# The low parts of eight weight tiles are made on GpSimd instead of VectorE, ahead of the output projection of a hybrid mixer

## The chip, the cores and the metric

The kernel runs on one core of a Trainium2 chip. A core has five engines that each work through their own list of instructions in order: TensorE (PE in the profile; PEld is its loading of weights), VectorE (DVE), ScalarE (ACT), GpSimd (POOL) and SyncE (SP), which here only starts transfers. They wait for each other by semaphores. The metric is the device time of one execution in microseconds, the median of several runs.

## The reference, cut to what matters

The reference is a decoder trunk of two layers for 512 tokens of width 1024. A layer is a SwiGLU block, a mixer and a second SwiGLU block, each with a scaled residual and a layer norm behind it:

```python
def hybrid_mixer(xn, w_in, conv_w, ..., w_out, lambda_init):
    qa, ka, va, qb, kb, vb, qkv_c, z_c, beta_c, a_c = jnp.split(xn @ w_in, points, axis=-1)
    ...
    oa = rms_norm(oa, diff_norm_g) * (1.0 - lambda_init)      # differential attention, 4 heads
    ob = rms_norm(ob, sb_norm_g)                              # stick-breaking attention, 4 heads
    oc = gated_delta_rule(l2_normalize(heads(qc, C_HEADS)), l2_normalize(heads(kc, C_HEADS)), ...)
    oc = rms_norm(oc, dn_norm_g) * jax.nn.silu(heads(z_c, C_HEADS).astype(jnp.float32))
    o = jnp.concatenate([tokens(oa), tokens(ob), tokens(oc)], axis=-1)
    return o @ w_out

    def step(state, inp):                                     # inside gated_delta_rule
        v_new = u_i - jnp.einsum('bhck,bhkv->bhcv', w_i, state)
        out = jnp.einsum(... q_i * exp(g_i), state) + jnp.einsum('bhcs,bhsv->bhcv', a_i, v_new)
        state = state * jnp.exp(g_last)[..., None] + jnp.einsum(... v_new)
        return state, out
```

The step carries a state from chunk to chunk and cannot run ahead of itself. The kernel uses chunks of 128 tokens, so there are four.

## The kernel before

All activations lie with features on the 128 partitions and the 512 tokens beside each other, as eight tiles of 128x512. Products with weights keep float32 accuracy with three passes: weights and activations are each split into a rounded high part and a low part (the rest), and `mm3` adds high times high (L103), high times low (L104) and low times high (L105).

`Stream.get` brings the weights. A transfer fetches eight blocks of 128x128 (`wraw`, two buffers); every four blocks are then split into `whi` by ScalarE (L89, a copy that rounds) and `wlo` (L90, a subtraction of two tensors in SBUF). Which engine runs L90 is decided by

```python
(eng or self.eng or nc.vector).tensor_tensor(out=lo, in0=r, in1=hi.bitcast(F32), op=ALU.subtract)
```

`st.eng` is None through the SwiGLU blocks, so DVE does it there. In the mixer it is set to `nc.gpsimd` after the first projections (L538) and, in the kernel before, set back to None at L1030, just before the output projection. The tiles come from the pools `ws` (six buffers) and `wx` (two at this point; its space is free only when the mixer's early pools are closed, L1031).

The mixer runs, in the order in which the code is written: projections and stick-breaking attention, projections of the delta rule with their convolution, the triangular inverses (`triangles`, `delta`), differential attention (`attend(0, 0)` and `attend(0, 1)`, units of scores L880/L881, softmax on ACT and DVE, L904 transposes, L909 products, and `finish` L948 to L966 with `turned` L972/L975 behind it), then `outputs`, which transposes the operands of the delta rule (`operands`, L758 and L763) and runs the scan. `gate` projects z and `split` (L994 on ACT, L995) makes high and low parts of the four attention outputs on GpSimd and of the four outputs of the delta rule on DVE; `nm.residual` adds the residual's high and low parts (L134, GpSimd).

The scan (`state`) works on two pairs of heads in turn. A step (`scan`) is L773 (PE), L775 (DVE), L779 (PE), L781 (DVE), L786 (PE), L792 (DVE, the new state; L789 in the first chunk), and L797 and L798 for the output, copied out by L840 (ACT). Its PSUM tiles come from a pool of two banks (`pa`). After every second chunk `emit` normalises a pair's outputs: L810 on ACT, then on DVE L814, L815, L816, a reciprocal root (L111, and three times L114, L115, L116 on tiles of 128x4 named `orr_t` and `of`), L818 and L819; a transpose (L824) follows at the next step. `finish` uses the same root (`arr_t`, `af`) for the attention.

The output projection (`project_norm` with `head`) works on four tiles of outputs first with the four attention parts as inputs, which can begin during the scan, then with the four parts of the delta rule; the low parts for these come by L90 of the first eight `get` groups. `nm.add` (L151 to L168) sums what the layer norm needs.

The order of instructions is not the order of the code. A scheduler places each engine's instructions by its own model of their durations, and an engine then keeps to that list. Thus an instruction that moves to another engine changes the lists of the others too.

Of the kernel before, what the change touches and what calls it, by code (L numbers as in the profile page):

```python
# [98 lines left out]
def mm3(g, out, w, x, first, last):  # L99
    nc = g.nc  # L100
    whi, wlo = w
    xhi, xlo = x
    nc.tensor.matmul(out=out, lhsT=whi, rhs=xhi, start=first, stop=False)  # L103
    nc.tensor.matmul(out=out, lhsT=whi, rhs=xlo, start=False, stop=False)  # L104
    nc.tensor.matmul(out=out, lhsT=wlo, rhs=xhi, start=False, stop=last)  # L105
# [321 lines left out]
def mixer(g, l):  # L427
    nc = g.nc
    st = g.st
# [12 lines left out]
    def pd():  # L442
        return g.pd.tile([P, T], F32, name="pd")

    def py():
        return psc.tile([P, T], F32, name="psc")
# [580 lines left out]
        nm.residual(d)  # L1027


    st.eng = st.queue = None  # L1030
    early.close()  # L1031
    g.more_weights()
    st.use([g.ws] * WS, [g.wx] * 2)
# [16 lines left out]
    def head():  # L1050

        tiles = [pd(), pd(), py(), py()]
        for a, b in ((0, 4), (4, KD)):
            for d, p in enumerate(tiles):
                for i in range(a, b):
                    mm3(g, p, st.get(bo + d * KD + order[i]), parts[i], i == 0, i == KD - 1)
                if b == KD:
                    for i in range(0, KD, PC):
                        st.get(bo + (d + 4) * KD + i)
                    nm.add(d, p, 0, T)  # L1060
            if b < KD:
                for d in range(4):
                    st.get(bo + d * KD + PC)
                st.use([g.ws] * 3 + [g.wx] * 5)

    def ahead(*pools):
# [6 lines left out]

    nxt = [st.at + i * PC for i in range(2 * NF)]
    project_norm(g, nm, ksum, False, 4, ((0, ahead(g.ws, g.ws, g.ws)), (KD, ahead(g.ws, g.ws)), (2 * KD, ahead(g.ws, g.wx)), (3 * KD, ahead(g.wx))), head, bank)
    ctx.close()


def program(ctx, tc, a, out, mixer=None):
# [101 lines left out]
    for l in range(DEPTH):  # L1181
        ffn(g, 3 * l, False, True)
        if mixer:
            mixer(g, l)
        ffn(g, 3 * l + 2, l == DEPTH - 1, False)
# [73 lines left out]
```

## Time and profile before

| | us |
|---|---|
| median of three runs | 2250.42 (2246.45 to 2251.85) |
| the profiled execution | 2250.16 |
| its span, first to last instruction | 2248.4 |
| PE busy | 2138.2 (95%) |
| DVE busy | 1169.6 (52%) |
| ACT busy | 907.9 (40%) |
| POOL busy | 377.5 (17%) |

The span of 2248.4 us holds both layers one after the other. The busy shares are means over stages with different limits; what a stage waits for is seen in the timelines, where a row has the start in us, the time that its instructions took, their line, operation and tiles, and, in brackets, the idle time of the engine before it with what ended that.

### The profile page before, as it was taken

The numbers are of one execution on the slowest core, as the hardware profiler recorded it, in microseconds if no ns is written. First come the engines' busy times: TensorE is split into PE (matmuls) and PEld (weight loads), VectorE is DVE, ScalarE is ACT, GpSimd is POOL, SyncE is SP. The second block draws the span as 40 slices with busy tenths as digits, with TensorE's granted clock in tenths as the row PEclk, the third lists the DMA queues.
The fourth block names the chain that finished last, engine by engine and source line by source line (L and its number), as shares of the span: only waits on it lengthen the run. The fifth ranks groups of instructions, "written<-read, shape, count | busy, mean of one in ns | idle before, by whom it ended". The sixth has DMA issues, their size and how long they took to land. (4 is left out here: it accounts for less than half of the span.)

```text
span 2248.4 us, 30132 instructions
## 1 busy us (share of the span) xinstructions
PE 2138.2 (95%) x11382; PEld 1782.6 (79%) x11382; DVE 1169.6 (52%) x2363; ACT 907.9 (40%) x1801; POOL 377.5 (17%) x327
## 2 busy tenths in 40 slices
PE   8999999999798999999999999999987989999997
PEld 7888889777677888888888888897776768888886
DVE  4533436386578833343663334263774788333426
ACT  4333324575464533332443333245753535333313
POOL 1100011426204400000130000023461234000010
PEclk9999999999899999999999999999998999999998
DMA  6423323514512233332333333234144123333322
GB/s 190 125 94 95 98 75 104 139 40 122 129 58 72 84 109 94 94 94 75 116 109 95 94 94 94 66 104 131 57 133 109 48 85 94 95 96 100 95 66 94
DMA packets 90898, 217.32 MB, mean 97 GB/s; under 512 B 21968, under 2 KB 36336, under 8 KB 90752
## 3 DMA queue, kind: packets, MB, share of 16 engines
q1 hardware_dynamic: 82848, 187.47, 27.5%
q10 hardware_dynamic: 6912, 25.17, 3.8%
q0 software_dynamic: 992, 2.75, 0.7%
q8 instruction: 90, 1.47, 0.3%
q14 instruction: 56, 0.46, 0.1%
HBM read 193.83 MB, written 6.83 MB: 89 GB/s over the span
## 5 line engine op out<-in xcount | busy, mean ns | idle before, releaser
L89 ACT CAST whi<-wraw 128x512 fp32r<-128x512 f32 x692 | 421.4, 619 | 959.4 <-PE pd L104 755.1
L90 DVE TENSOR_TENSOR wlo<-wraw,whi 128x512 fp32r<-128x512 f32 x580 | 431.0, 751 | 658.6 <-ACT whi L89 647.4
L103 PE MATMUL pd<-x,whi 128*128 128x512 f32 (+1 forms) x1920 | 726.7, 380 | 12.9 <-ACT x L1177 6.2
L105 PE MATMUL pd<-x,wlo 128*128 128x512 f32 (+1 forms) x1920 | 728.3, 380 | 3.2 <-DVE wlo L90 3.2
L104 PE MATMUL pd<-x,whi 128*128 128x512 f32 (+1 forms) x1920 | 727.7, 379 | 1.6 <-POOL x L231 1.3
L103 PEld LDWEIGHTS pd<-x,whi 128*128 128x128 f32 x1920 | 365.8, 191 | 77.5 <-ACT x L1177 6.2
L105 PEld LDWEIGHTS pd<-x,wlo 128*128 128x128 f32 x1920 | 366.2, 191 | 67.4 <-DVE wlo L90 3.4
L104 PEld LDWEIGHTS pd<-x,whi 128*128 128x128 f32 x1920 | 366.2, 191 | 66.8 <-POOL x L231 3.0
L103 PE MATMUL pd<-hhi,whi 128*128 128x512 f32 (+1 forms) x880 | 307.7, 350 | 0.0
L104 PE MATMUL pd<-hlo,whi 128*128 128x512 f32 (+1 forms) x880 | 307.7, 350 | 0.0
L105 PE MATMUL pd<-hhi,wlo 128*128 128x512 f32 (+1 forms) x880 | 307.3, 349 | 0.0
L168 POOL TENSOR_TENSOR lt<-lt 128x512 f32<-128x512 f32 x26 | 38.9, 1497 | 1065.3 <-ACT lt L165 1065.3
L103 PEld LDWEIGHTS pd<-hhi,whi 128*128 128x128 f32 x880 | 165.5, 188 | 24.4
L105 PEld LDWEIGHTS pd<-hhi,wlo 128*128 128x128 f32 x880 | 165.4, 188 | 24.1
L104 PEld LDWEIGHTS pd<-hlo,whi 128*128 128x128 f32 x880 | 165.5, 188 | 24.1
L90 POOL TENSOR_TENSOR wlo<-wraw,whi 128x512 fp32r<-128x512 f32 x112 | 150.2, 1357 | 138.7 <-ACT whi L89 70.1
L259 DVE TENSOR_TENSOR lt<-pd,lt 128x512 f32<-128x512 f32 x88 | 60.4, 689 | 111.9 <-PE pd L105 110.7
L231 POOL TENSOR_TENSOR x<-x 128x256 fp32r<-128x256 f32 x60 | 45.1, 753 | 162.5 <-ACT x L229 132.7
L134 POOL TENSOR_TENSOR x<-x 128x512 f32<-128x512 f32 x48 | 70.9, 1522 | 0.0
L261 DVE TENSOR_TENSOR hlo<-lt,hhi 128x512 fp32r<-128x512 f32 x88 | 67.0, 765 | 6.3
L165 ACT ACTIVATE lt<-x 128x256 f32<-128x256 f32 (+1 forms) x58 | 29.7, 512 | 95.8 <-DVE x L163 95.5
L568 DVE SCALAR_TENSOR_TENSOR kqv<-pd,conv,kqv 128x511 f32<-128x511 f32 (+2 forms) x72 | 53.5, 743 | 20.1 <-ACT kqv L566 18.9
(309 smaller groups left out, 2287.9 us busy)
## 6 DMA issues: line engine op xcount, KB each, us to landing
wraw<-in_w SPq DMA_DIRECT2D x308, 512.0 KB, 3.5
wraw<-in_w ACTq DMA_DIRECT2D x48, 512.0 KB, 3.6
kqv<-kqv SPq DMA_DIRECT2D x128, 64.0 KB, 2.0
kqv<-kqv SPq DMA_DIRECT2D x48, 128.0 KB, 4.7
scr<-zero POOLq DMA_DIRECT2D x2, 1032.0 KB, 11.1
x<-in_xT SPq DMA_DIRECT2D x8, 256.0 KB, 5.5
scr<-inv SPq DMA_DIRECT2D x8, 256.0 KB, 2.7
XT<-scr SPq DMA_DIRECT2D x8, 256.0 KB, 4.8
```

Source lines behind the costliest of these rows:

```text
L89: nc.scalar.copy(out=hi, in_=r)
L90: (eng or self.eng or nc.vector).tensor_tensor(out=lo, in0=r, in1=hi.bitcast(F32), op=ALU.subtract)
L103: nc.tensor.matmul(out=out, lhsT=whi, rhs=xhi, start=first, stop=False)
L104: nc.tensor.matmul(out=out, lhsT=whi, rhs=xlo, start=False, stop=False)
L105: nc.tensor.matmul(out=out, lhsT=wlo, rhs=xhi, start=False, stop=last)
L134: i = g.nc.gpsimd.tensor_tensor(out=t, in0=xhi.bitcast(F32), in1=xlo.bitcast(F32), op=ALU.add)
L165: nc.scalar.activation(out=sq[:, r], in_=t[:, r], func=AF.Square)
L168: eng.tensor_tensor(out=self.acc2[:, r], in0=self.acc2[:, r], in1=sq[:, r], op=ALU.add)
L231: eng.tensor_tensor(out=xlo[:, r], in0=t[:, r], in1=xhi[:, r].bitcast(F32), op=ALU.subtract)
L259: nc.vector.tensor_tensor(out=sg, in0=pu, in1=sg, op=ALU.mult)
L261: nc.vector.tensor_tensor(out=hlo, in0=sg, in1=hhi.bitcast(F32), op=ALU.subtract)
L568: nc.vector.scalar_tensor_tensor(out=y[:, s:], in0=p[:, :T - s], scalar=wc[:, 3 - s:4 - s], in1=y[:, s:], op0=ALU.mult, op1=ALU.add)
```

## The change

`st.eng` is no longer set back ahead of the output projection but in the middle of `head`, after the first eight groups of four blocks have been asked for. These eight L90 in each layer run on GpSimd; the later ones run on VectorE as before (and those of `ahead` on GpSimd as before).

```diff
-    st.eng = st.queue = None
+    st.queue = None
     early.close()
     g.more_weights()
     st.use([g.ws] * WS, [g.wx] * 2)
...
             if b < KD:
                 for d in range(4):
                     st.get(bo + d * KD + PC)
+                st.eng = None
                 st.use([g.ws] * 3 + [g.wx] * 5)
```

On GpSimd, from the clearing of the blocks of the inverse (L695, L696) to the second block's layer norm, the list of instructions changes like this; L90 makes `wlo`, L995 the low parts of the attention outputs, L134 the residuals, L168 sums of squares. The place is the end of the mixer of a layer:

```order
 L695 MEMSET blk 128x256
 L696 MEMSET blk 128x16
-L90 TENSOR_TENSOR wlo<-wraw,whi 128x512 x2
+L90 TENSOR_TENSOR wlo<-wraw,whi 128x512 x8
 L995 TENSOR_TENSOR kqv<-x,kqv 128x256 x8
 L134 TENSOR_TENSOR x<-x 128x512 x8
-L168 TENSOR_TENSOR lt<-lt 128x512 x3
-L90 TENSOR_TENSOR wlo<-wraw,whi 128x512 x8
+L90 TENSOR_TENSOR wlo<-wraw,whi 128x512 x2
+L168 TENSOR_TENSOR lt<-lt 128x512 x2
+L90 TENSOR_TENSOR wlo<-wraw,whi 128x512
+L168 TENSOR_TENSOR lt<-lt 128x512
```

Six of the eight stand ahead of the splits L995 (the two that were there make weights of the last gate), two behind the residuals L134.

On PE the scan begins elsewhere in the list. In the kernel before, the first products of the scan (L779, then L786 and L798 of chunk 0) stand between the units of the attention (L909, L904, L880, L881):

```order
L881 MATMUL psc<-maskb,identb 128x128
L904 MATMUL pt<-ident,at 128x128 x2
L798 MATMUL pa<-vn,intra 128x128
L779 MATMUL pa<-inv,XT 128x128 x2
L104 MATMUL pd<-x,whi 128x512
L105 MATMUL pd<-x,wlo 128x512
L909 MATMUL po<-kqv,at 128x64 x2
L904 MATMUL pt<-ident,at 128x128
L786 MATMUL pa<-vn,inv 128x128 x2
```

In the changed kernel the last transposes of operands (L758, L763), four gate matmuls (`pd<-x`) and nearly all of the attention stand ahead of the first L779:

```order
L904 MATMUL pt<-ident,at 128x128 x2
L758 MATMUL pa<-ident,kqv 128x128 x4
L763 MATMUL pa<-ident,kqv 128x128 x4
L105 MATMUL pd<-x,wlo 128x512
L103 MATMUL pd<-x,whi 128x512
L104 MATMUL pd<-x,whi 128x512
L105 MATMUL pd<-x,wlo 128x512
L909 MATMUL po<-kqv,at 128x64 x2
L904 MATMUL pt<-ident,at 128x128
L779 MATMUL pa<-inv,XT 128x128 x2
L103 MATMUL pd<-x,whi 128x512
L104 MATMUL pd<-x,whi 128x512
```

So the scan starts later in PE's list, with more of the gate's matmuls left for its steps.

On DVE the finish of the attention (L966, which `turned`, the splits L994 and L995 and then the residuals wait for) moves against the two emissions of the scan. In the kernel before it stands behind the greater part of the first emission (`orr_t`, `of`), whose L818 and L819 follow, with the second emission already begun (L814, L815, L816):

```order
L815 SCALAR_TENSOR_TENSOR oms<-oms,sq_3659 128x4
L964 TENSOR_TENSOR af<-af,ars 128x8
L114 TENSOR_TENSOR orr_t<-of 128x4
L816 TENSOR_SCALAR oms<-oms 128x4
L966 TENSOR_TENSOR at<-at,af 128x512
L115 SCALAR_TENSOR_TENSOR orr_t<-orr_t,oms 128x4
L111 TENSOR_SCALAR of<-oms 128x4
L775 SCALAR_TENSOR_TENSOR inv<-pa,neG,inv 128x128
L116 SCALAR_TENSOR_TENSOR of<-orr_t,of 128x4
L114 TENSOR_TENSOR orr_t<-of 128x4
L818 TENSOR_TENSOR of<-of,sqs 128x4
```

In the changed kernel it stands ahead of both, directly behind the new state (L792) of the pair's second chunk:

```order
L964 TENSOR_TENSOR af<-af,ars 128x8
L792 SCALAR_TENSOR_TENSOR S<-S,eG,pa 128x128
L966 TENSOR_TENSOR at<-at,af 128x512
L775 SCALAR_TENSOR_TENSOR inv<-pa,neG,inv 128x128
L814 TENSOR_REDUCE oms<-lt 128x4
L775 SCALAR_TENSOR_TENSOR inv<-pa,neG,inv 128x128
L815 SCALAR_TENSOR_TENSOR oms<-oms,sq_3659 128x4
L816 TENSOR_SCALAR oms<-oms 128x4
L111 TENSOR_SCALAR of<-oms 128x4
L114 TENSOR_TENSOR orr_t<-of 128x4
L781 TENSOR_TENSOR vn<-pa,brk 128x256
```

Both emissions, with 24 operations on two operands in SBUF, now come after L966; in the kernel before 15 of them did.

## Rows read from the trace of the kernel before

**Rows 1.** Busy time of each engine by stretch, end of the mixer, layer 0.

```profile
core 0: us, PE busy (x) PEld busy (x) DVE busy (x) ACT busy (x) POOL busy (x), PEclk, DMA share, GB/s
603.00:638.60 35.60, 33.07 (x318) 25.11 (x317) 16.31 (x42) 18.95 (x48) 0.00 (x0) 0.97 0.41 112
638.60:652.80 14.20, 14.20 (x115) 11.37 (x114) 10.61 (x29) 4.86 (x13) 0.00 (x0) 1.00 0.29 90
652.80:661.00 8.20, 8.20 (x71) 7.60 (x70) 5.80 (x21) 6.36 (x19) 0.00 (x0) 1.00 0.06 22
661.00:679.00 18.00, 14.69 (x96) 11.90 (x95) 15.54 (x63) 10.89 (x27) 6.15 (x9) 1.00 0.10 31
```

**Rows 2.** Timeline of PE: start us, us, line, operation; steps of the scan.

```profile
652.84 0.66 PE L779 MATMUL pa<-inv,XT 128*128 128x128 f32 x4
...
660.90 0.71 PE L773 MATMUL pa<-S,kqv 128*128 128x128 f32 x4
...
662.20 0.63 PE L779 MATMUL pa<-inv,XT 128*128 128x128 f32 x4
...
664.79 0.68 PE L773 MATMUL pa<-S,kqv 128*128 128x128 f32 x4
...
669.59 0.61 PE L773 MATMUL pa<-S,kqv 128*128 128x128 f32 x4
...
672.42 0.66 PE L972 MATMUL pt<-ident,at 128*128 128x128 f32 x4 [0.30 <-DVE at L966]
...
677.25 0.61 PE L773 MATMUL pa<-S,kqv 128*128 128x128 f32 x4
...
682.71 0.71 PE L773 MATMUL pa<-S,kqv 128*128 128x128 f32 x4
...
697.75 0.60 PE L824 MATMUL pa<-ident,o 128*128 128x128 f32 x4
```

**Rows 3.** Timeline of POOL: splits and residuals, layer 0.

```profile
674.32 4.16 POOL L995 TENSOR_TENSOR kqv<-x,kqv 128x256 fp32r<-128x256 f32 x6 [6.93 <-ACT kqv L994]
678.43 10.38 POOL L134 TENSOR_TENSOR x<-x 128x512 f32<-128x512 f32 x8
...
765.19 13.49 POOL L134 TENSOR_TENSOR x<-x 128x512 f32<-128x512 f32 x8
```

**Rows 4.** Timeline of DVE: operations beside POOL's.

```profile
674.27 0.16 DVE L115 SCALAR_TENSOR_TENSOR orr_t<-orr_t,oms 128x4 f32<-128x4 f32 x1
674.47 0.59 DVE L116 SCALAR_TENSOR_TENSOR of<-orr_t,of 128x4 f32<-128x4 f32 x1
...
677.84 1.19 DVE L819 TENSOR_TENSOR o<-o,of 128x512 f32<-128x512 f32 x1
678.96 0.59 DVE L775 SCALAR_TENSOR_TENSOR inv<-pa,neG,inv 128x128 f32<-128x128 f32 x2
...
688.13 0.70 DVE L815 SCALAR_TENSOR_TENSOR oms<-oms,sq 128x4 f32<-128x4 f32 x1
...
765.44 5.19 DVE L90 TENSOR_TENSOR wlo<-wraw,whi 128x512 fp32r<-128x512 f32 x3
770.55 1.28 DVE L259 TENSOR_TENSOR lt<-pd,lt 128x512 f32<-128x512 f32 x2
```

**Rows 5.** Timeline of DVE: L90 in the scan and behind it, and L966.

```profile
667.84 0.68 DVE L90 TENSOR_TENSOR wlo<-wraw,whi 128x512 fp32r<-128x512 f32 x1
...
671.69 0.68 DVE L966 TENSOR_TENSOR at<-at,af 128x512 f32<-128x512 f32 x1
...
701.44 1.29 DVE L90 TENSOR_TENSOR wlo<-wraw,whi 128x512 fp32r<-128x512 f32 x2
```

**Rows 6.** Page, costliest groups: L90 on DVE and on POOL.

```profile
L90 DVE TENSOR_TENSOR wlo<-wraw,whi 128x512 fp32r<-128x512 f32 x580 | 431.0, 751 | 658.6 <-ACT whi L89 647.4
...
L90 POOL TENSOR_TENSOR wlo<-wraw,whi 128x512 fp32r<-128x512 f32 x112 | 150.2, 1357 | 138.7 <-ACT whi L89 70.1
```

## The prediction

> **What bounds the kernel now.** I read the page first, then the busy time by stretch, then the timelines of VectorE (DVE), GpSimd (POOL) and TensorE (PE) through the mixer of layer 0; layer 1 runs the same instructions in the same order, so every sum is doubled. PE is the bound of the whole kernel. The place of the change is the mixer's end, and there the stretches differ [rows 1]: from 603 to 638.6 us PE is busy 33.07 of 35.60 us and from there to 652.8 all of 14.20, with other projections as filling. From 661 to 679, inside the scan of the delta rule, it is busy 14.69 of 18.00 while DVE is busy 15.54: here PE waits for DVE.
>
> The scan is a chain of steps, one for each pair of heads (A is heads 0 and 1, B is 2 and 3) and each chunk. Only two `pa` banks serve it, so the steps follow one another. The reader sees their starts in the L773 rows [rows 2]: A1 (pair A, chunk 1) at 660.90, B1 664.79, A2 669.59, B2 677.25, A3 682.71; chunk 0 starts at the first L779 (652.84), and the last turning of an output (L824) starts at 697.75. A1 takes 3.9 us. A2 takes 7.7. The difference is DVE's: between the steps' own operations, which read PSUM, the order puts the long runs of small operations that normalise outputs (`emit`, L814 to L819).
>
> What makes these runs slow is seen on POOL. POOL splits the attention outputs (L995) from 674.32 and makes the residual sums (L134) from 678.43 to 688.81, back to back [rows 3]. A small DVE operation with both tensors in SBUF takes 0.16 us at 674.27 and 0.59 us at the next operation, once L995 is on [rows 4]. L819 at 677.84 takes 1.19 us, and L815 at 688.13 takes 0.70 us and ends at 688.83, as POOL's last L134 ends (688.81). Operations with one operand in PSUM pay nothing: two L775 at 678.96 take 0.59 together while L134 runs. With full-size operands, eight L134 take 13.49 us (1.69 each, against 1.30 in the mixer) while DVE's L90 take 5.19 for three; two L259, from PSUM, take 1.28 [rows 3, 4]. So the two engines alternate, one whole instruction each, when DVE's operation has two SBUF inputs.
>
> The Trainium skill, "SBUF — State Buffer", section "Who interferes with whom", says that such an instruction contends with a POOL instruction that reads SBUF, and that the one that starts first holds the shared port pair to its end. It speaks against this change: by it each L90 that goes to POOL can hold up DVE for longer than it relieves it. The rows above agree.
>
> **The change part by part.** *Removed from DVE:* eight L90 for each layer. Two back to back take 1.29 us at 701.44 [rows 5], so one costs DVE 0.60; together 4.8 us. On the path lie few: five ran before 652.8, where PE has filling, and are worth nothing. One at 667.84 (0.60) and the two at 701.44 (1.2) are worth at most 1.8.
>
> *Added to POOL:* eight L90 at about 1.3 us (the page's mean for POOL is 1.357 us against 0.751 on DVE [rows 6]). POOL has nothing to do from 603 to 661 [rows 1], so nothing queues there behind the first five. What they cost is one blocked DVE operation each; four of these hits PE's filling hides, the fifth falls on an L926 of the attention and I take 0.7 us for it. The sixth stands in POOL's order directly ahead of L995, the seventh and eighth behind L134.
>
> *Moved:* the order of PE and DVE changes, and this is the larger part. I walk through the new order with durations of the old trace; times are those of layer 0.
>
> First, the transposes of the operands (L758, L763) go between the attention's pieces, and the rest of the attention goes in front of the first L779. PE did this attention work between 652.8 and 661.0, busy all 8.20 us [rows 1]; by the starts of its rows some 4.6 us of it is attention. Four gate matmuls (1.0 us) go the other way. With the 0.7 above, the first L779 moves from 652.84 to 652.84 + 4.6 − 1.0 + 0.7 ≈ 657.2.
>
> Chunk 0 then runs without attention between its steps: a step like A1 without L773 and L775 is 3.9 − 1.3 (660.90 to 662.20) = 2.6, two are 5.3. A1 starts at 662.5, 1.6 us later than before.
>
> In A1 now stands the finish of the attention (L953 to L966). Its small operations meet L90 number six and the first two L995: I count three hits and 1.5 us in all. B1 starts at 662.5 + 3.9 + 1.5 = 667.9 (before: 664.79).
>
> L966 now ends at about 668.3, ahead of both emissions. In the old trace L966 starts at 671.69 and the L995 run follows at 674.32, 2.6 us later, through L972 at 672.42 and ScalarE [rows 2, 3, 5]. That link is kept. But there 9 of the remaining 15 two-operand operations were through by then, and 6 met L995 (not L134). Now 24 two-operand operations stand behind L966. From about 670.2 POOL runs six L995 (0.69 each, 4.16 for six) and eight L134 (1.30 each, 10.38 for eight), and DVE gets one small operation through per POOL instruction. So about six emission operations of A end with the L995 (674.4), the next with the first L134 (675.6), and the second L792 of B1, on which A2's start waits, stands behind them: A2 starts at 675.9 (before: 669.59). Four more of A's (L115, L116, L818, L819) end with L134 number two to five, plus 0.6 for L819 itself: 681.4. Only then comes A2's L775. B's L815, L114 and L115 end with L134 six to eight: 685.2. After that DVE is free: four small operations, two L792 and the rest take 2.7, B2 starts at about 687.5 (before: 677.25).
>
> From there no POOL work is in the way. B2 loses the hit on L819 and the wait behind it, 4.1 instead of 5.5, so A3 starts at 691.6 (before: 682.71). From A3 to the last L824 the old trace takes 15.04; without the hit on L815 (0.55) it is 14.5: 706.1 against 697.75. The scan ends 8.35 us later.
>
> *The tail.* L90 seven and eight follow when the banks of weights come free, beside L1025 and L995 of the second half of the mixer's outputs. DVE is relieved of 1.2. If both hit an L995, PE gets these operands up to 2 × 1.26 = 2.5 later. Bounds −1.2 and +1.3 for each layer; neither row is nearer, I take 0. What follows the tail (matmuls of the second half, the norm) is unchanged in amount and shifts with it.
>
> The sum is 2 × 8.35 = 16.7 us. The profiled execution took 2250.16 us (span 2248.4), the median of the runs is 2250.42, so they are one and the same here: 2250.2 + 16.7 = 2266.9. For the walk itself the bounds are +1.3 (rival two) and +10.5 for each layer (every one of the fourteen POOL instructions holds a small operation, and A1 loses another 1.5 to the L90 and pays the tail's hits in part).
>
> **The rivals.** *One: DVE is simply relieved, and the kernel is faster.* For it: DVE is busy 15.54 of 18.00 us where PE waits, and the new order puts filling matmuls between the steps. If the port cost nothing more than before, the 1.8 us on the path go: 2 × 1.8 = 3.6, 2246.6 us; were all 4.8 on the path, 2240.6. It decides if small operations seldom meet POOL, that is if L966 comes so late that both emissions are through. Against it: the new DVE order has L966 ahead of them. The Trainium skill, "Perfetto Trace Analysis", section "Optimizing Scalar/DVE Operations", allows moving work to GpSimd when DVE is saturated, and adds that between these two it might not help; the first half of that would give this rival's time.
>
> *Two: hits, but no more than before.* If emission A is through before L995 starts (because ScalarE brings L994 later), B meets six L995 as in the old trace. Then the scan loses 1.6 + 1.5 − 0.6, about 2.5, and the tail gives 1.2 back: 1.3 for each layer, 2252.8 us, no measurable change. For it: the old trace had just this pattern. Against it: L994 hangs on L972 alone, whose place in PE's order is directly behind B1's L773.
>
> *Three: the start decides.* If the hits are half of what I count (about 4 us) and only the later start and A1's loss (3.1) stay, the scan ends some 4 to 5 us late, 2259 us.
>
> **How the numbers follow.** The forecast has 0.58, with a range of its own from 2261 to 2274. Rival three 0.14, two 0.16, one 0.12. A measurement of this kernel tells about 0.3% (6.75 us) from no change. The forecast and most of three are slower by more than that: 0.70. Two, the rest of three and the on-path form of one are within it: 0.22. Faster by more needs nearly all eight L90 on the path: 0.08. The range that holds 8 in 10 leaves out most of one and the far end of the walk: 2249 to 2275.
>
> **What would show it.** Right: in the scan of the changed trace L115, L116 and L114 of the `orr_t` runs take about 1.3 us each beside L134, A2 to B2 takes over 10 us, the last L824 comes some 8 us later relative to the double stage, and PE idles before L779 of A2. Right for the first step: L773 of A1 within 2 us of its old place. Wrong: the `orr_t` operations at 0.16 us, or L134 starting only after the second L819; then rival one or two holds. Also wrong would be a POOL run broken by waits for buffers, which would let DVE through in between.

## The result and the profile after

The changed kernel takes 2270.58 us (median of 5 runs, 2268.36 to 2273.66); the kernel before took 2248.22 us beside it (2245.77 to 2251.85). The ratio is 1.0100, 95% interval 1.0085 to 1.0115: slower by 19 to 26 us, about 22, where 16.7 were predicted. The profiled execution has a span of 2266.8 us against 2248.4.

PE's busy time by stretch, as in [rows 1] (the last column but two is the mean granted clock of TensorE, 1.00 being 2.4 GHz):

```profile
core 0: us, PE busy (x) PEld busy (x) DVE busy (x) ACT busy (x) POOL busy (x), PEclk, DMA share, GB/s
661.00:679.00 18.00, 11.39 (x60) 9.05 (x58) 15.50 (x35) 6.39 (x16) 11.62 (x13) 0.91 0.09 30
698.00:709.00 11.00, 8.60 (x33) 5.81 (x31) 8.07 (x33) 4.44 (x11) 0.00 (x0) 0.84 0.00 0
```

From 661 to 679 PE is busy 11.39 us where it was busy 14.69 [rows 1], POOL 11.62 instead of 6.15. The granted clock fell too: 0.91 in this stretch and 0.84 in the second, which holds the scan's end and part of what follows, where the kernel before had 1.00 from 661 to 703. The steps of the scan are on PE's timeline, answering to [rows 2]:

```profile
654.84 0.61 PE L779 MATMUL pa<-inv,XT 128*128 128x128 f32 x4
...
660.51 0.64 PE L773 MATMUL pa<-S,kqv 128*128 128x128 f32 x4
...
667.63 0.70 PE L773 MATMUL pa<-S,kqv 128*128 128x128 f32 x4
...
675.73 0.71 PE L773 MATMUL pa<-S,kqv 128*128 128x128 f32 x4 [2.17 <-DVE S L792]
...
681.26 0.56 PE L779 MATMUL pa<-inv,XT 128*128 128x128 f32 x2 [3.88 <-DVE inv L775]
...
687.18 0.66 PE L773 MATMUL pa<-S,kqv 128*128 128x128 f32 x4
...
703.62 0.73 PE L103 MATMUL pd<-kqv,whi 128*128 128x512 f32 x2 [2.03 <-ACT kqv L994]
...
705.84 1.06 PE L105 MATMUL pd<-kqv,wlo 128*128 128x512 f32 x2
706.70 1.06 PE L824 MATMUL pa<-ident,o 128*128 128x128 f32 x4
```

B1 to A2 (667.63 to 675.73) and A2 to B2 (675.73 to 687.18) have grown, and at both PE waits for DVE: 2.17 us for S, 3.88 us for an L775. POOL's row over the same time, answering to [rows 3]:

```profile
670.02 4.16 POOL L995 TENSOR_TENSOR kqv<-x,kqv 128x256 fp32r<-128x256 f32 x6 [6.16 <-ACT kqv L994]
674.14 10.31 POOL L134 TENSOR_TENSOR x<-x 128x512 f32<-128x512 f32 x8
709.22 1.51 POOL L90 TENSOR_TENSOR wlo<-wraw,whi 128x512 fp32r<-128x512 f32 x1 [24.76 <-ACT whi L89]
```

L995 starts 4.3 us earlier than before (2.7 counted from the memset of the table below) and the residual sums follow at once. What they meet on DVE answers to [rows 4]:

```profile
669.89 0.17 DVE L111 TENSOR_SCALAR of<-oms 128x4 int32<-128x4 int32 x1
...
674.38 1.04 DVE L114 TENSOR_TENSOR orr_t<-of 128x4 f32<-128x4 f32 x1
675.34 0.34 DVE L792 SCALAR_TENSOR_TENSOR S<-S,eG,pa 128x128 f32<-128x128 f32 x1
...
677.92 1.19 DVE L818 TENSOR_TENSOR of<-of,sqs 128x4 f32<-128x4 f32 x1
679.14 1.71 DVE L819 TENSOR_TENSOR o<-o,of 128x512 f32<-128x512 f32 x1
...
682.07 1.18 DVE L816 TENSOR_SCALAR oms<-oms 128x4 f32<-128x4 f32 x1
...
684.51 0.16 DVE L114 TENSOR_TENSOR orr_t<-of 128x4 f32<-128x4 f32 x1
```

L111 takes 0.17 us at 669.89, before POOL begins. From L114 (1.04 us) to L818 (1.19) each of four operations ends with a sum on POOL, L819 (1.71) waits for the fifth sum and then runs, and L816 of pair B (1.18) ends with a sum too. L792, with one operand in PSUM, takes 0.34 in the midst of it. When POOL is done, at 684.45, L114 is back at 0.16.

A table over both layers is the best ledger. It counts from the last memset on POOL ahead of the scan (L696: 575.51 and 1689.62 us before, 573.93 and 1697.96 after), so that what a layer inherits from earlier ones falls out: start is from there to the first L779, scan from there to the last L824, tail from there to L151. Values are layer 0 / layer 1, in us; ratios are to the kernel before, timed beside each. The median of first six only leaves out one execution of 3010.8 us, which ran at a granted clock of 0.65.

| kernel | median | ratio (95% interval) | start | scan | tail |
|---|---|---|---|---|---|
| before | 2248.2 | 1 | 77.3 / 77.8 | 44.9 / 44.9 | 4.9 / 4.9 |
| after | 2270.6 | 1.0100 (1.0085 to 1.0115) | 80.9 / 81.6 | 51.9 / 50.4 | 7.3 / 7.3 |
| sums late | 2258.9 | 1.0045 (1.0033 to 1.0058) | 80.9 / 81.9 | 46.2 / 44.6 | 7.8 / 7.8 |
| order alone | 2264.9 | 1.0068 (1.0054 to 1.0082) | 78.1 / 77.3 | 53.3 / 51.5 | 4.9 / 4.9 |
| L966 put back | 2269.0 | 1.0088 (1.0075 to 1.0102) | 82.2 / 81.6 | 49.7 / 49.5 | 6.9 / 6.9 |
| first six only | 2266.0 | 1.0092 (1.0079 to 1.0105) | 80.7 / 82.1 | 51.8 / 50.5 | 5.4 / 5.4 |
| last two only | 2249.9 | 1.0012 (1.0003 to 1.0022) | 77.3 / 77.7 | 44.9 / 44.9 | 6.9 / 7.3 |
| after, PSUM | 2255.8 | 1.0042 (1.0030 to 1.0054) | 81.7 / 81.2 | 42.7 / 44.3 | 6.9 / 7.2 |
| before, PSUM | 2245.9 | 0.9995 (0.9986 to 1.0003) | 78.1 / 77.7 | 43.8 / 43.8 | 4.9 / 4.9 |
| six and PSUM | 2253.0 | 1.0013 (1.0003 to 1.0023) | 82.1 / 81.4 | 42.7 / 44.3 | 4.9 / 4.9 |

In the changed kernel the three columns have grown by 12.9 us in layer 0 and 11.7 in layer 1. The single profiled execution shows 18.4 in its span. From layer 0's first L231 to layer 1's memset it took 944.1 us against 947.9 before; the other kernels, which change nothing there, take 942.1 to 946.8, so most of that difference may be scatter between executions. Another 2.2 come back between L151 and L231 of layer 1 (39.2 against 41.4, the others 38.6 to 41.2), which was not followed up.

### The profile page after: what moved, and what is told of

Read it like the earlier page. It is cut to its first block, busy times and chain, and to the rows that moved or that the text cites. A ratio compares the mean times of both kernels' runs of the same rounds, so it can differ in the third digit from the quotient of the medians.

```text
span 2266.8 us, 30126 instructions
## 1 busy us (share of the span) xinstructions
PE 2143.1 (95%) x11382; PEld 1784.1 (79%) x11382; DVE 1189.4 (52%) x2347; ACT 907.7 (40%) x1801; POOL 400.9 (18%) x343
## 4 chain that ended last, share of the span: by engine, by line
PE 74%; DVE 15%; DMA 4%; ACT 3%; issue 3%; POOL 1%; SPq 0%; ACTq 0%; POOLq 0%; DVEq 0%
PE pd L105 22%; PE pd L104 22%; PE pd L103 22%; DMA wraw<-in_w 3%; DVE wlo L90 2%; PE po L909 1%; ACT whi L89 1%; DVE x L212 1%; DVE at L939 1%; DVE kqv L568 1%; DVE x L220 1%; PE psc L880 1%; PE pt L904 1%; DVE lt L166 0%; DVE at L940 0%
## 5 line engine op out<-in xcount | busy, mean ns | idle before, releaser
L90 DVE TENSOR_TENSOR wlo<-wraw,whi 128x512 fp32r<-128x512 f32 x564 | 421.9, 756 | 639.1 <-ACT whi L89 630.4
L103 PE MATMUL pd<-x,whi 128*128 128x512 f32 (+1 forms) x1920 | 725.6, 379 | 12.9 <-ACT x L1178 6.3
L105 PE MATMUL pd<-x,wlo 128*128 128x512 f32 (+1 forms) x1920 | 726.0, 378 | 2.5 <-DVE wlo L90 2.4
L103 PEld LDWEIGHTS pd<-x,whi 128*128 128x128 f32 x1920 | 364.8, 190 | 76.9 <-ACT x L1178 6.3
L105 PEld LDWEIGHTS pd<-x,wlo 128*128 128x128 f32 x1920 | 365.2, 190 | 67.0 <-DVE wlo L90 2.7
L103 PE MATMUL pd<-hhi,whi 128*128 128x512 f32 (+1 forms) x880 | 307.7, 350 | 0.0
L105 PE MATMUL pd<-hhi,wlo 128*128 128x512 f32 (+1 forms) x880 | 307.3, 349 | 0.0
L90 POOL TENSOR_TENSOR wlo<-wraw,whi 128x512 fp32r<-128x512 f32 x128 | 171.4, 1352 | 315.1 <-ACT whi L89 214.5
L168 POOL TENSOR_TENSOR lt<-lt 128x512 f32<-128x512 f32 x26 | 41.0, 1575 | 1036.5 <-ACT lt L165 1036.4
L103 PEld LDWEIGHTS pd<-hhi,whi 128*128 128x128 f32 x880 | 165.4, 188 | 24.4
L105 PEld LDWEIGHTS pd<-hhi,wlo 128*128 128x128 f32 x880 | 165.4, 188 | 24.2
L231 POOL TENSOR_TENSOR x<-x 128x256 fp32r<-128x256 f32 x60 | 45.1, 752 | 159.0 <-ACT x L229 156.4
L134 POOL TENSOR_TENSOR x<-x 128x512 f32<-128x512 f32 x48 | 71.2, 1534 | 0.0
```

What stands on the lines that cost most here:

```text
L134: i = g.nc.gpsimd.tensor_tensor(out=t, in0=xhi.bitcast(F32), in1=xlo.bitcast(F32), op=ALU.add)
L168: eng.tensor_tensor(out=self.acc2[:, r], in0=self.acc2[:, r], in1=sq[:, r], op=ALU.add)
L231: eng.tensor_tensor(out=xlo[:, r], in0=t[:, r], in1=xhi[:, r].bitcast(F32), op=ALU.subtract)
```

## The experiments

**Which operations are held.** A kernel that only measures: rows of VectorE instructions, alone, beside GpSimd tensor_tensor, beside GpSimd memsets.

> Leaves the whole computation out: eight forms of VectorE instructions (tensor_tensor, scalar_tensor_tensor, tensor_scalar, copy, reduce of 128x512, two with one operand in PSUM, all with 128x4 results, and a tensor_tensor of 128x512), each run alone, then beside a row of eight GpSimd tensor_tensor of 128x512 that read SBUF, then beside eight GpSimd memsets of 128x512. My theory (the two engines alternate whole instructions where VectorE's has two SBUF inputs): tensor_tensor and scalar_tensor_tensor from SBUF rise from about 0.16 to 1.0 us or more beside the GpSimd tensor_tensor, the forms with one input, the reduce and those with PSUM stay within 0.1 us; tensor_scalar is open, since L816 and L111 took 1.18 and 1.19 us in the changed kernel. The memsets read nothing and hold nobody up. Rival (SBUF is simply busy): every form that touches SBUF, the reduce above all, takes some 10 to 50% longer, and the small ones hardly change.

Its timeline: first eight of each form alone (the eight forms start from 4.75 to 19.90 us), then sixteen beside eight instructions of POOL (L49 tensor_tensor, L50 memset). L39 is a tensor_tensor from SBUF, L41 a tensor_scalar, L43 a reduce, L44 a tensor_tensor with one input in PSUM:

```profile
4.75 1.53 DVE L39 TENSOR_TENSOR sc<-sa,sb 128x4 f32<-128x4 f32 x8
...
25.59 10.84 DVE L39 TENSOR_TENSOR sc<-sa,sb 128x4 f32<-128x4 f32 x16
25.75 10.66 POOL L49 TENSOR_TENSOR sink<-big,big 128x512 f32<-128x512 f32 x8 [25.31 <-DVE sc L39]
...
47.64 10.91 DVE L41 TENSOR_SCALAR sc<-sa 128x4 f32<-128x4 f32 x16
...
69.63 11.49 DVE L43 TENSOR_REDUCE sc<-big 128x4 f32<-128x512 f32 x16
...
81.24 3.10 DVE L44 TENSOR_TENSOR sc<-acc,sb 128x4 f32<-128x4 f32 x16
...
122.17 3.12 DVE L39 TENSOR_TENSOR sc<-sa,sb 128x4 f32<-128x4 f32 x16
...
131.78 6.21 DVE L41 TENSOR_SCALAR sc<-sa 128x4 f32<-128x4 f32 x16
```

Sixteen tensor_tensor from SBUF last as long as POOL's eight instructions (10.84 against 10.66); sixteen with one input in PSUM take 3.10, as undisturbed (1.53 for eight in either form); sixteen reduces take 11.49 against 5.73 for eight, undisturbed too. So the alternation holds and the rival (SBUF simply busy) falls. Tensor_scalar, left open, is held as well, and also by memsets (6.21), which leave tensor_tensor alone (3.12). The Trainium skill, "SBUF — State Buffer", section "Who interferes with whom", says just this: two SBUF inputs contend with a GpSimd instruction that reads SBUF and not with one that only writes; copy and tensor_scalar can enter a mode that takes both ports; a reduce never contends. These rows agree on each point. Three points of the expectation missed: copy, with one input, is held like tensor_scalar (10.91 for sixteen); memsets do hold these two (6.21 and 6.17 for sixteen, where eight alone take 1.60); and a held form costs 0.68 us in the mean (10.84 / 16), not 1.0, since one held operation (1.11) and one free (0.16, with 0.04 of idle time) pass for each instruction of POOL.

**The sums held back.** The changed kernel in its own order; only a wait is added, on the L819 of the second emission.

```diff
-        nm.residual(d)
+        nm.residual(d, marks[1])      # marks: the L819 of each emission; residual waits for it
```

> The changed kernel with its instruction order untouched on every engine; only the first of the eight residual sums (L134) waits until the second emission's L819 is through. My theory (the sums hold the emissions' small operations): L134 comes off L114, L115, L116, L818 and L819 of pair A (1.04, 1.05, 1.20, 1.19 and 1.71 us) and off L816 and L111 of pair B; by the walk A2's L779 comes at about 677.4 instead of 681.26, B2 at about 681 instead of 687.18, one or two operations of the third emission are then hit, so the last L824 comes at about 701.5 instead of 706.70. Two layers give 10 us: about 2257 (2253 to 2260). Rival (the changed start and the eight L90 on GpSimd cost the time): no gain, 2266 to 2272, or worse by the wait.

The timeline of DVE in this kernel, at the places of the changed kernel's L114 and L819 of pair A:

```profile
674.53 0.15 DVE L114 TENSOR_TENSOR orr_t<-of 128x4 f32<-128x4 f32 x1
...
675.45 0.69 DVE L819 TENSOR_TENSOR o<-o,of 128x512 f32<-128x512 f32 x1
```

And of PE, the start of B2 and the last L824:

```profile
680.56 0.66 PE L773 MATMUL pa<-S,kqv 128*128 128x128 f32 x4
...
701.11 1.05 PE L824 MATMUL pa<-ident,o 128*128 128x128 f32 x4
```

L114 takes 0.15 us instead of 1.04, L819 0.69 instead of 1.71; B2 starts at 680.56 and the last L824 at 701.11, as worked out. The time is 2258.87, 11.7 us below the changed kernel. The eight sums alone cost about 6 us a layer, with nothing else moved.

**The order alone.** The kernel before, all L90 on VectorE; the emissions' first reduce is ordered behind L966 (no wait is added, only the order of DVE and PE).

```diff
-        nc.vector.tensor_reduce(out=msf, in_=sq, ...)
+        g.after(nc.vector.tensor_reduce(out=msf, in_=sq, ...), marks[-1])   # marks[-1]: L966
```

> The kernel before, all L90 of the output weights on VectorE; only the order is changed: both emissions of the first two chunks stand behind L966, as in the changed kernel. My theory (L966 ahead of the emissions lets L995 and L134 collide with their small operations): some 18 of the 24 two-operand operations are left when L995 starts at about 673.6, six end with an L995 and eight with an L134, L775 of B2 waits for them until about 688, and the last L824 is 7 to 9 us late in each layer: 2262 to 2268. Rival (GpSimd's eight L90 are what costs the time, order costs nothing): 2245 to 2251.

The timeline of DVE, once POOL is at L134 (677.48 to 688.23):

```profile
677.58 1.20 DVE L115 SCALAR_TENSOR_TENSOR orr_t<-orr_t,oms 128x4 f32<-128x4 f32 x1
678.70 0.15 DVE L114 TENSOR_TENSOR orr_t<-of 128x4 f32<-128x4 f32 x1
678.80 1.19 DVE L116 SCALAR_TENSOR_TENSOR of<-orr_t,of 128x4 f32<-128x4 f32 x1
679.91 0.15 DVE L115 SCALAR_TENSOR_TENSOR orr_t<-orr_t,oms 128x4 f32<-128x4 f32 x1
...
684.14 1.73 DVE L819 TENSOR_TENSOR o<-o,of 128x512 f32<-128x512 f32 x1
685.80 0.60 DVE L775 SCALAR_TENSOR_TENSOR inv<-pa,neG,inv 128x128 f32<-128x128 f32 x2
```

2264.94 us, with none of the eight L90 on POOL: the place of L966 is enough for the collision, without the load that POOL was given. Here the two emissions alternate, and each held operation of one is followed by a free one of the other (1.20, 0.15, 1.19, 0.15). Yet L775 of B2 waits until 685.80, and the scan is 8.4 and 6.6 us longer, 6.9 of it from A2 to B2 in either layer.

**L966 put back.** The changed kernel with L966 ordered behind the L819 of emission A. This is further back than in the kernel before, where it stood ahead of A's L818 and L819 and behind B's L815.

```diff
-        nc.vector.tensor_tensor(out=o, in0=o, in1=last(ff, P), op=ALU.mult)
+        i = nc.vector.tensor_tensor(out=o, in0=o, in1=last(ff, P), op=ALU.mult); hp[0] == cs[0] == 0 and g.after(marks[-1], i)
```

> The changed kernel, its eight L90 on GpSimd; only L966 is put back behind the emission of pair A, as it stood in the kernel before. My theory: emission A is through before L995 starts, emission B meets six L995 and at most three L134, the last L824 falls back from 706.70 to about 698 to 700; what stays is the start of A1 and the tail: 2249 to 2257. Rival (the eight L90 on GpSimd cost the time wherever L966 stands): 2264 to 2272.

The timeline of DVE: L819 of pair A, then L115 and L819 of pair B.

```profile
672.97 0.69 DVE L819 TENSOR_TENSOR o<-o,of 128x512 f32<-128x512 f32 x1
...
680.57 1.05 DVE L115 SCALAR_TENSOR_TENSOR orr_t<-orr_t,oms 128x4 f32<-128x4 f32 x1
...
684.10 1.72 DVE L819 TENSOR_TENSOR o<-o,of 128x512 f32<-128x512 f32 x1
```

The timeline of PE: A2, the L779 of B2, and A3.

```profile
672.72 0.60 PE L773 MATMUL pa<-S,kqv 128*128 128x128 f32 x4
...
686.22 1.19 PE L779 MATMUL pa<-inv,XT 128*128 128x128 f32 x4 [3.24 <-DVE inv L775]
...
691.90 0.68 PE L773 MATMUL pa<-S,kqv 128*128 128x128 f32 x4
```

And the busy time from there to A3, with the columns of [rows 1]:

```profile
681.80:692.00 10.20, 6.96 (x28) 5.88 (x27) 5.50 (x8) 0.80 (x3) 8.82 (x7) 0.50 0.00 0
```

A miss: 2268.97. Emission A is free now (L819 at 672.97 takes 0.69), and A2 starts at 672.72 instead of 675.73. But emission B begins only behind L966, and its operations meet the six L995 and then four L134 (1.05, 1.20, 1.18, 1.72): B2's L779 waits 3.24 us. A second cause adds to it: from 681.8 to 692.0 the granted clock is 0.50, and from B2's L779 to A3 the same matmuls take 5.68 us where they take 3.26 in the changed kernel (688.39 to 691.65). So A3 starts at 691.90, nearly as in the changed kernel. In the kernel before the two emissions alternate, and six of B's twelve two-operand operations were through when L995 began. My count of "at most three" sums overlooked that. The time is the rival's, but in the rows POOL runs L995 and L134 there and no L90; what is lost is lost to these and to the clock.

**The two ends of the change apart.** Only the first six L90 on GpSimd (edit of the changed kernel, shown), and only the last two (the same edit of the kernel before, with `nc.gpsimd` for `nc.vector`).

```diff
                 for d in range(4):
-                    st.get(bo + d * KD + PC)
+                    st.get(bo + d * KD + PC, eng=nc.vector if d > 1 else None)
```

> The changed kernel with only the first six of the eight L90 on GpSimd; the last two, which follow the residual sums, go back to VectorE. The order through the scan stays as in the changed kernel, the tail is that of the kernel before. From the changed trace the stretch from the last L824 to the first L179 is 34.5 us against 31.1 before, 3.4 us more in each layer. My theory now (the scan costs most, but the tail, which I had put at nothing, costs some 3 us a layer as well): 2261 to 2267, about 2264. Rival (the tail costs nothing, as I had predicted): 2268 to 2273.

> The kernel before with only the last two of the eight L90 on GpSimd: the order of the scan is that of the kernel before, only the tail is changed. My theory now (the tail alone costs some 3 us a layer: both L90 hold up L995 on VectorE, and PE waits for them): 2252 to 2257, about 2255. Rival (the tail costs nothing): 2246 to 2251.

The first lies in its range (2266.0), though its ratio (1.0092) cannot be told from the changed kernel's (1.0100); the second lies below its range and in the rival's (2249.85). The timeline of DVE in the tail of the kernel before:

```profile
700.10 1.43 DVE L995 TENSOR_TENSOR kqv<-x,kqv 128x256 fp32r<-128x256 f32 x4
...
702.65 0.68 DVE L151 SCALAR_TENSOR_TENSOR x<-x,pd 128x512 f32<-128x512 f32 x1
```

And with the last two on GpSimd:

```profile
697.88 3.61 DVE L995 TENSOR_TENSOR kqv<-x,kqv 128x256 fp32r<-128x256 f32 x4
702.39 0.69 DVE L151 SCALAR_TENSOR_TENSOR x<-x,pd 128x512 f32<-128x512 f32 x1 [0.90 <-PE pd L105]
```

Four L995 take 3.61 us instead of 1.43 beside two L90 of 1.5 us on POOL, and the tail grows by 2.0 and 2.4 us. In time that gives 2.7 us (0.7 to 4.9) over both layers, an interval that holds the rows' 4.4. With the two L90 back on VectorE the tail falls from 7.3 to 5.4. The first six, and the order that came with them, cost the bulk.

**The port taken out of the way.** The emissions' small tensors go into a PSUM bank that is idle in the scan, and Newton's products are ordered so that each operation reads one of them there. POOL's work stays where it is.

```diff
-        ms = sm.tile([P, n, 2], F32, name="oms")
-        f = sm.tile([P, n, 2], F32, name="of")
+        ms, f = (ep[0][:, i:i + 2 * n].rearrange("p (h c) -> p h c", c=2) for i in (k, k + 8))   # ep[0]: pav "po"
...
-        nc.vector.tensor_tensor(out=t, in0=out, in1=out, op=ALU.mult)
-        nc.vector.scalar_tensor_tensor(out=t, in0=t, scalar=-0.5, in1=x, op0=ALU.mult, op1=ALU.mult)
+        nc.vector.scalar_tensor_tensor(out=t, in0=out, scalar=-0.5, in1=x, op0=ALU.mult, op1=ALU.mult)
+        nc.vector.tensor_tensor(out=t, in0=t, in1=out, op=ALU.mult)
```

> The changed kernel, with all GpSimd work where it is, but the emissions' small tensors (oms, of) in a PSUM bank that is idle in the scan, and Newton's products in an order in which each reads one of them, so that no emission operation but L111 has all its inputs in SBUF. The number and kinds of instructions stay. My theory (it is the shared port and nothing else): L114, L115, L116, L818 take about 0.2 us and L819 0.7 beside L995 and L134, A2 starts at about 672 to 673 instead of 675.73, B2 at 677 to 679 instead of 687.18, the last L824 at about 698 instead of 706.70; what stays is A1's start and hits and the tail: 2249 to 2256, about 2252, below the kernel in which only the residual sums wait. Rival (the operations are late for another reason: the start, the order, GpSimd's load): 2264 to 2272.

The timeline of DVE, two operations of emission A beside POOL's L995 and L134:

```profile
673.02 0.16 DVE L115 TENSOR_TENSOR orr_t<-orr_t,po 128x4 f32<-128x4 f32 x1
...
674.20 0.68 DVE L819 TENSOR_TENSOR o<-o,po 128x512 f32<-128x512 f32 x1
```

And of PE, B2 and the last L824:

```profile
677.79 0.67 PE L773 MATMUL pa<-S,kqv 128*128 128x128 f32 x4
...
698.64 0.60 PE L824 MATMUL pa<-ident,o 128*128 128x128 f32 x4
```

L115 at 673.02 takes 0.16 and L819 at 674.20 takes 0.68, though POOL runs L995 and L134 from 669.58 to 683.63. A2, B2 and the last L824 come where they were worked out, and the scan (42.7 and 44.3) is shorter than before the change. The time, 2255.82, lies at the upper end of what I expected. POOL's work is the same, and the held operations run free beside it: that is the port. How much of the scan's gain is the port alone is less sure, since the order moved a little too: some gate matmuls trade places, and on VectorE A2's L775 now stands ahead of A's L818 and L819, no longer behind them. The kernel with the sums held back, in which no engine's order moved through the scan, shows the same cause without that doubt. What is left is start and tail.

The same edit in the kernel before, and with the last two L90 back on VectorE:

> The kernel before with the emissions' small tensors in the same idle PSUM bank. My theory: the six hits by L995 (2.6 us), the one on L819 (0.5) and the one on L815 (0.55) go, 3 to 3.6 us a layer, of which the order's other waits take some back: 2241 to 2246, a version faster than both kernels. Rival (these hits are hidden behind other waits, or the PSUM operands are slower themselves): 2247 to 2252.

> Both remedies in the changed kernel: the emissions' small tensors in the idle PSUM bank, and the last two of the eight L90 back on VectorE. Theory: nothing of the collisions is left but those in A1; per layer the later first L779 stays (3.7 us in the changed trace, counted from the same memset), the scan from there to the last L824 is 1 to 2 us shorter than before, the tail 0.5 longer: 2 to 3 us a layer, 2251 to 2255 where the kernel before takes 2247 to 2249, and 2 to 4 us below the kernel with the PSUM bank alone. Rival (once the emissions are free, eight L90 less on VectorE pay): at or below the kernel before, 2240 to 2249.

Before with PSUM: 0.9995 (0.9986 to 1.0003), no difference that can be measured. Its median, 2245.90, is in the expected range, but the kernel before took 2247.05 beside it: it was to beat both kernels and does not. Its scan is 1.1 us shorter in each layer, not 3. Why is open: those hits may have lain beside other waits, and VectorE's order moved too (emission B begins only behind A's L819). With six and PSUM: 2253.01, as expected, 1.0013 (1.0003 to 1.0023). With the emissions' collisions and the tail's gone, the change still gives nothing: the later start (4.7 and 3.6 us) eats the shorter scan (2.2 and 0.6).

## Why the prediction was right

Direction and mechanism held. Its steps against the trace, in us between one step and the next:

| from, to | before | predicted | after, layer 0 | layer 1 |
|---|---|---|---|---|
| memset, first L779 | 77.3 | 81.7 | 80.9 | 81.6 |
| first L779, A1 | 8.1 | 5.3 | 5.7 | 5.7 |
| A1, B1 | 3.9 | 5.4 | 7.1 | 5.6 |
| B1, A2 | 4.8 | 8.0 | 8.1 | 8.0 |
| A2, B2 | 7.7 | 11.6 | 11.5 | 11.4 |
| B2, A3 | 5.5 | 4.1 | 4.5 | 4.5 |
| A3, last L824 | 15.0 | 14.5 | 15.1 | 15.2 |
| last L824, L151 | 4.9 | 4.9 | 7.3 | 7.3 |

- *The collision (B1 to B2).* Worked out to 0.2 us. That L966 ahead of the emissions is enough to cause it is shown by the order alone (2264.9), and that the port is its means by the sums held back (L114 0.15 us, L819 0.69, order untouched) and the PSUM kernel (scan 42.7 and 44.3). Part of the exactness is luck: the walk had B's L815, L114 and L115 end with the last three sums. In the trace L815 ran free (0.15), L819 delayed the sixth sum (1.73 us), and the last two sums held L816 and L111, which have one SBUF input and should have passed by the prediction's rule.
- *The later start.* 3.6 and 3.8 us instead of 4.4, of which the shorter chunk 0 takes 2.4 back (2.8 forecast). It is read from PE's order; that part of the order was not tried alone.
- *A1.* The three hits came as counted: in layer 1 A1 takes 5.6. In layer 0 the matmuls L797 and L798 took 0.64 instead of 0.39 us behind three short waits of PE (0.44, 0.75 and 0.93 us): by then the granted clock was 0.50 from 664.4 to 667.8, which I had not counted.
- *A3 to the end.* I had taken off 0.5 us for the hit on L815; the stretch kept its 15 us. The rows show the 0.5 and what took it back: the first L103 behind PE's last wait comes 11.97 us after A3 instead of 12.56, but from it to the last L824 it takes 3.08 us instead of 2.48, since the granted clock is 0.50 from 705.4 to 708.8 (two L105 at 705.84 take 1.06 us, 0.63 in the kernel before).
- *The tail.* The mis-sized term: taken at nothing between −1.2 and +1.3, it is 2.4 us by the rows; in time 1.4 a layer (0.4 to 2.5) by the last two alone. Of the 2.4, the L90 cost 1.95, from the L1025 behind the last L824 to L151 (5.71 us against 3.76): both do hit an L995, and PE waits in turn for wlo (0.85) and kqv (0.72). The other 0.46 lie ahead of that L1025 and are the clock's (L824 takes 1.06 us instead of 0.60); first six only, with the two L90 on DVE, keeps these alone (tail 5.4). The relief of 1.2 on DVE did not show.

Against the forecast the two layers lost 4.6 and 3.4 us more: the tail (2.4 each), A1 in layer 0 (1.7), A3 to the end (0.6 and 0.7) and small terms, less the start's 0.8 and 0.6. Of this the lower clock is, by these rows, some 2.6 in layer 0 and 1.2 in layer 1, a cost that the prediction has nowhere. In its walk two sums are slightly off: two steps of 2.6 us make 5.2, not 5.3, and the last sum ends at 684.8 by its own terms (674.4 and 10.38), not 685.2; the 687.5 for B2 goes by 684.8.

Rival one falls with the time, and its price with the kernel of six and PSUM: even with the emissions' hits gone, DVE's relief doesn't show. Rivals two and three fall with the rows: thirteen of the fourteen POOL instructions (six L995, eight L134) hold an operation each.

## What to carry to other kernels

Before work goes from VectorE to GpSimd, look in the new order at what each GpSimd instruction will run beside: a chain of small dependent operations with both tensors in SBUF paid one GpSimd instruction per operation here. The cost may lie far from the moved work, because the scheduler moves other instructions when an engine is relieved. If such a chain must run there, keep one operand of each operation in PSUM, or make the GpSimd work wait for its end; in these runs either took back much of the loss, and neither made the change pay.

## What the runs showed of the hardware that I had not expected

- Small tensor_scalar and copy from SBUF to SBUF are held too: L816 and L111 took 1.18 and 1.19 us beside L134, and sixteen took 10.91 us beside eight GpSimd tensor_tensor, and 6.21 beside memsets.
- One or two operations pass for each GpSimd instruction, and the rows show when. In the changed kernel each L134 starts 0.04 us before the last one ends and a dependent operation 0.03 to 0.04 us after the one it reads from: one passes. With the order alone, L114 of the other emission starts at 678.70, before the held L115 ends (678.77) and just ahead of the next L134 (678.71), and runs free (0.15): two pass. In the measuring kernel GpSimd's instructions stand 0.08 us apart, and one free operation (0.16) follows each held one (1.11).
- A small operand in PSUM cost nothing: eight tensor_tensor of 128x4 take 1.53 us with it and without it.
- What VectorE loses, PE can lose a second time to its clock. In the kernel before the granted clock is 1.00 through the scan of layer 0. In the changed kernel it is 0.50 (1.2 GHz) in three stretches there: from 664.4, at the end of waits of 0.44, 0.75 and 0.93 us, from 681.5, behind 2.17 and 3.88, and from 705.4, behind 2.03. With L966 put back it is 0.50 from 681.8 to 692.0, and B2's L779 took 1.19 us, where the four at 654.84 in the changed kernel took 0.61.
